# A hybrid mLSTM and sparse-attention block: the first stage's work in another order

## The chip, the core and the metric

The kernel runs on one core of a Trainium2 chip. The core has a matrix engine (TensorE, PE in the profile, with its weight loads as PEld), three engines for elementwise work (VectorE or DVE, ScalarE or ACT, GpSimd or POOL) and a queue for transfers (SyncE, SP). Each engine works through its own queue of instructions in order and waits on semaphores for the others. The time is device time in microseconds from one execution; the metric is the median of several executions.

## The reference

One decoder block of width 1024 on 512 tokens. It normalises the input, projects it with one wide matrix, and feeds the columns of that projection to two branches:

```
hN = rmsnorm(x, norm_g)
p  = split(hN @ w_in)          # m_q m_k m_v m_o m_z m_i m_f | n_q n_kc n_vc n_ks n_vs n_kw n_vw n_g n_z | g_a g_b
mLSTM branch:  conv + silu of q, k; chunkwise matrix memory with input gate m_i and forget gate m_f; layer norm
NSA branch:    compressed, selected and window attention over n_kc/n_vc, n_ks/n_vs, n_kw/n_vw, gated by n_g
merged = sigmoid(g_a) * (ya @ w_branch_a) + sigmoid(g_b) * (yb @ w_branch_b)
out    = rmsnorm(x + merged @ w_out, final_norm_g)
```

All tensors are float32. What matters here is the beginning: the norm of x, its transpose, and the projection onto a few narrow columns (n_vs, n_vw, n_g, m_i, m_f: 288 columns together).

## The kernel before

A float32 product is made of three products in a faster number format: each operand is split into a high part, which is the value rounded by a copy, and a low part, which is the value less its high part. `split` (line 129) does this with a copy on ACT and a subtraction on DVE. `mm3` (line 156) and `passes` (line 199) then issue high by high, high by low and low by high for every 128-row slice k of the contraction (eight slices, ND).

The first stage (lines 249 to 368) handles the 512 tokens in four blocks `tb` of 128. For each block:

- `stats(tb)`: ACT squares x and sums the squares (`ssq`), takes a logarithm (`ln`) and an exponential (`r`); one Newton step of four or five small instructions refines the inverse root, on DVE for block 0 and on POOL (lines 301 to 307) for the others.
- `transposed(tb)`: in two halves of 512 columns, DVE scales x in place by r and the norm's weight `gB` (tile `xt`), and TensorE transposes four slices into a bank of PSUM (tile `pt`, two banks).
- in the loop, `split` makes `hTh` (ACT) and `hTl` (DVE) from each half; `mm3` projects the block with 24 products of 288 columns (tile `pp`).
- `evacuate(tb, ps)` brings a finished projection out of PSUM: two pairs of an ACT copy and a DVE subtraction (tile `vsw`), then two DVE additions (tile `gp`) of biases.

The 288 columns of the weights arrive in tile `sraw` and are split two slices at a time by `small_split(k)` into `shi` and `slo`: for k = 0 and 4 POOL makes the high part and DVE the low part, for k = 2 and 6 ACT makes the high part and POOL the low part.

What sets the order: while the set `ordered` holds "act" and "dve", everything issued to those two engines keeps its order in the program; TensorE's, POOL's and SP's instructions are placed by a planner, which interleaves the transposes of the next block with the projection of the current one. The projection of block `tb` is issued after the next block's `transposed`, so on DVE the scaling of block tb + 1 stands ahead of `evacuate(tb - 1)`. After the stage `ordered.clear()` (line 368) hands ACT and DVE to the planner as well.

The loads of the first weights of the wide columns follow on SP's queue (line 143, tiles `wr`, `wh`, `wl`), each a job of the `Stream`: first two jobs for the compressed keys and values, then two for the selected and window keys. Behind them stand small transposes of parameters (L385, L386, L389), the angles of the rotary embedding (sine) and the forget gate's logarithm (tiles `fa`, `fe`, `fz`, `lf`). Tiles of the next stage reuse the memory of the first: the load of `w1t` (line 509), which the compression's first product (L537) reads together with `X`, waits until the last user of that memory is done.

Of the kernel before, what the change touches and what calls it, by code (L numbers as in the profile page):

```python
# [15 lines left out]
OP = mybir.AluOpType  # L16
# [4 lines left out]
NT = T // 128  # L21
ND = D // 128
# [41 lines left out]
def build(  # L64
# [4 lines left out]
    nc = tc.nc  # L69
# [17 lines left out]
    pe, pool = nc.tensor, nc.gpsimd  # L87
    act, dve = Engine(nc.scalar, "act"), Engine(nc.vector, "dve")
# [25 lines left out]
    ident = cst[:, CI : CI + 128]  # L114
# [41 lines left out]
    def mm3(ps, lh, ll, rh, rl, ks, start=True, stop=True):  # L156
        n = len(ks)
        for i, k in enumerate(ks):
            a, b, c, d = lh(k), ll(k), rh(k), rl(k)
            pe.matmul(ps, a, c, start=start and i == 0, stop=False)  # L160
            pe.matmul(ps, a, d, start=False, stop=False)  # L161
            pe.matmul(ps, b, c, start=False, stop=stop and i == n - 1)  # L162
# [71 lines left out]
    hTh = pers.tile([128, ND, T], F32R, name="hTh")  # L234
    hTl = pers.tile([128, ND, T], F32R, name="hTl")
# [13 lines left out]
    with tc.tile_pool(name="ph0", bufs=2, side="right") as p0, tc.tile_pool(  # L249
        name="small", bufs=1, side="right"  # L250
    ) as sp:
        SW = 288
        xts = [p0.tile([128, D], F32, name="xt", tag="xt", bufs=4) for _ in range(NT)]
# [7 lines left out]
        for k in (0, 4):  # L261
            ks = slice(k, k + 4)
# [9 lines left out]
        gB = []  # L272
        for hf in range(2):
            ps = PS()
            pe.matmul(ps, one, grow[:, hf * 512 : hf * 512 + 512], start=True, stop=True)
            gB.append(ps)
        shi = sp.tile([128, ND, SW], F32R, name="shi")
        slo = sp.tile([128, ND, SW], F32R, name="slo")

        def small_split(k):  # L280
            ks = slice(k, k + 2)
            if k % 4:
                A(shi[:, ks], raw[:, ks], AF.Copy)
# [3 lines left out]
            eng.tensor_tensor(slo[:, ks], raw[:, ks], f(shi[:, ks]), OP.subtract)  # L287

        epst = p0.tile([128, 1], F32, name="epst", bufs=1)
# [1 line left out]
        ssq = p0.tile([128, NT], F32, name="ssq", bufs=1)  # L291
        rs = []

        def stats(tb):
            sq = p0.tile([128, D], F32, name="sq", tag="sq", bufs=1)
            A(sq, xts[tb], AF.Square, accum_out=ssq[:, tb : tb + 1])
            v = p0.tile([128, 1], F32, name="v", tag="v", bufs=4)
            ln = p0.tile([128, 1], F32, name="ln", tag="ln", bufs=4)
            A(ln, ssq[:, tb : tb + 1], AF.Ln, bias=epst[:, 0:1], scale=1.0 / D)
            e = pool if tb else dve  # L300
# [3 lines left out]
            e.tensor_tensor(v, r, v, OP.mult)  # L304
            e.tensor_tensor(v, r, v, OP.mult)
# [19 lines left out]
        stats(0)  # L325

        def transposed(tb):
            xt, pts = xts[tb], []
            for hf in range(2):
                hs = slice(hf * 512, hf * 512 + 512)  # L330
                dve.scalar_tensor_tensor(xt[:, hs], xt[:, hs], rs[tb][:, 0:1], gB[hf], OP.mult, OP.mult)
                ps = PT()
                for k in range(4):
                    kk = hf * 4 + k
                    pe.transpose(ps[:, k * 128 : (k + 1) * 128], xt[:, kk * 128 : (kk + 1) * 128], ident)
                pts.append(ps.rearrange("p (k t) -> p k t", k=4))
            return pts

        pts = transposed(0)
        small_split(0)  # L340
        small_split(2)
        stats(1)
        last = None
        for tb in range(NT):
            ts = slice(tb * 128, (tb + 1) * 128)
            for hf in range(2):
                ks = slice(hf * 4, hf * 4 + 4)
                split(pts[hf], hTh[:, ks, ts], hTl[:, ks, ts])
                if tb == 0:
                    small_split(4 + 2 * hf)  # L350
# [11 lines left out]
            if tb == 0:  # L362
                nc.sync.dma_start(bif[:, 0:4], b_igate[0].partition_broadcast(128))
                nc.sync.dma_start(bif[:, 4:8], b_fgate[0].partition_broadcast(128))
                nc.sync.dma_start(bng, b_nsa_gate[0].partition_broadcast(128))
        stream.fetch()
        evacuate(NT - 1, last)
        ordered.clear()
# [14 lines left out]
        ps = PT()  # L383
# [13 lines left out]
        kk = sp.tile([128, 2, NT, 8], F32, name="kk")  # L397
# [277 lines left out]
    for src, dst in ((cpad, Ct), (spad, St)):  # L675
        ps = PT()
# [265 lines left out]
    for h in range(4):  # L942
# [54 lines left out]
        r = rsqrt(mp, va, NT, "rl")  # L997
# [26 lines left out]
    with tc.tile_pool(name="fin", bufs=1) as fp:  # L1024
# [106 lines left out]
```

## Time and profile before

| what | value |
|---|---|
| median of 3 runs | 645.48 us (644.75 to 646.33) |
| profiled execution | 644.24 us, its span 642.4 us |
| TensorE busy | 626.9 us, 98% of the span |
| VectorE, ScalarE, GpSimd busy | 411.5, 302.4, 54.0 us |
| granted TensorE clock, mean | 0.998 of full speed |
| bytes read from and written to memory | 55.01 MB, 2.10 MB |

The span runs from the first to the last instruction on the core; all times below that are not durations are counted from its start. In a row of the timeline stand the start, the duration, the engine, the line, the operation and the tiles written and read, with "xN" where N instructions are merged, and in brackets the idle time before them with what ended it. The chain of waits follows the work that ended last back from the end; its rows hold a start and the time that the step adds. L80 is the line of the helper through which all of ACT's and DVE's work passes, so their instructions are told apart by their tiles.

### The profile page before, as it was taken

How to read it: one execution, taken by the hardware profiler on the slowest of the kernel's cores; microseconds unless marked ns; L12 is line 12 of the kernel's file. 1: busy time of each engine (PE TensorE's matmuls, PEld its weight loads, DVE VectorE, ACT ScalarE, POOL GpSimd, SP SyncE). 2: the span in 40 equal slices, each digit the busy share in tenths (PEclk: the TensorE clock that was granted, in tenths of full speed). 3: DMA queues.
4: the chain of work that ended last, by engine and by line, in shares of the span. 5: the costliest groups of instructions: out<-in, count | busy, mean ns of one | idle time of the engine just before them, and what ended most of it. 6: DMA issues, size and time to landing. Idle time of an engine off the chain costs nothing.

```text
span 642.4 us, 9274 instructions
## 1 busy us (share of the span) xinstructions
PE 626.9 (98%) x3470; PEld 538.8 (84%) x3470; DVE 411.5 (64%) x878; ACT 302.4 (47%) x604; POOL 54.0 (8%) x114
## 2 busy tenths in 40 slices
PE   6999999999999999999999999999999999999995
PEld 4988788888878788888989889889888888888995
DVE  5796768767866865557669788696554233334455
ACT  5653554655655655435545546545322222223234
POOL 5000021121121231100000000000000000000000
PEclk9999999999999999999999999999999999999999
DMA  8476421122122212223313222232274242423203
GB/s 248 136 193 154 120 66 45 55 67 67 36 64 66 65 49 83 66 70 96 99 37 96 80 73 78 67 78 87 66 232 128 66 131 67 128 70 108 90 1 131
DMA packets 90124, 58.74 MB, mean 91 GB/s; under 512 B 4016, under 2 KB 86100, under 8 KB 90080
## 3 DMA queue, kind: packets, MB, share of 16 engines
q1 hardware_dynamic: 90080, 58.16, 31.8%
q8 instruction: 27, 0.44, 0.3%
q14 instruction: 17, 0.14, 0.1%
HBM read 55.01 MB, written 2.10 MB: 89 GB/s over the span
## 4 chain that ended last, share of the span: by engine, by line
PE 88%; DVE 7%; ACT 2%; DMA 1%; issue 1%; SPq 0%; POOL 0%; DVEq 0%; POOLq 0%
PE pp L204 21%; PE pp L202 21%; PE pp L206 21%; PE pp L162 3%; PE pp L160 3%; PE pp L161 3%; PE pt L784 2%; DVE wl L80 2%; PE po L797 1%; PE ps L769 1%; PE po L796 1%; PE ps L537 1%; ACT wh L80 1%; PE ps L770 1%; PE ps L162 1%
## 5 line engine op out<-in xcount | busy, mean ns | idle before, releaser
L202 PE MATMUL pp<-hTh,wh 128*128 128x512 f32 (+1 forms) x488 | 192.2, 394 | 0.0
L204 PE MATMUL pp<-hTl,wh 128*128 128x512 f32 (+1 forms) x488 | 191.3, 392 | 0.0
L206 PE MATMUL pp<-hTh,wl 128*128 128x512 f32 (+1 forms) x488 | 191.1, 392 | 0.0
L80 DVE TENSOR_TENSOR wl<-wr,wh 128x1024 fp32r<-128x1024 f32 x88 | 109.0, 1240 | 74.3 <-ACT wh L80 73.9
L80 ACT ACTIVATE wh<-wr 128x1024 fp32r<-128x1024 f32 x88 | 92.9, 1057 | 114.3 <-PE pp L204 82.8
L206 PEld LDWEIGHTS pp<-hTh,wl 128*128 128x128 f32 x488 | 91.8, 188 | 16.2
L202 PEld LDWEIGHTS pp<-hTh,wh 128*128 128x128 f32 x488 | 92.0, 188 | 15.3
L204 PEld LDWEIGHTS pp<-hTl,wh 128*128 128x128 f32 x488 | 92.0, 189 | 15.1
L778 POOL TENSOR_SCALAR P<-P,st 128x128 f32<-128x128 f32 (+1 forms) x64 | 38.5, 620 | 182.2 <-DVE st L80 134.1
L80 ACT ACTIVATE P<-P,st 128x128 f32<-128x128 f32 (+3 forms) x64 | 35.7, 558 | 36.6 <-DVE st L80 36.4
L80 DVE CUSTOM_DVE_ANT_0 P<-ps,cst 128x128 f32<-128x128 f32 (+3 forms) x64 | 30.4, 486 | 22.0 <-PE ps L770 21.6
L80 ACT ACTIVATE pth<-pt 128x512 fp32r<-128x512 f32 (+1 forms) x64 | 27.2, 434 | 29.8 <-PE pt L784 18.6
L80 DVE TENSOR_TENSOR ptl<-pt,pth 128x512 fp32r<-128x512 f32 (+1 forms) x64 | 30.4, 484 | 16.4 <-ACT pth L80 15.7
L204 PE MATMUL pp<-wl,hTh 128*128 128x256 f32 x128 | 36.2, 283 | 0.0
L206 PE MATMUL pp<-wh,hTl 128*128 128x256 f32 x128 | 36.2, 283 | 0.0
L202 PE MATMUL pp<-wh,hTh 128*128 128x256 f32 x128 | 36.2, 283 | 0.0
L161 PE MATMUL pp<-wl,meh 128*128 128x256 f32 x128 | 36.2, 283 | 0.0
L160 PE MATMUL pp<-wh,meh 128*128 128x256 f32 x128 | 36.2, 283 | 0.0
L162 PE MATMUL pp<-wh,mel 128*128 128x256 f32 x128 | 36.2, 284 | 0.0
L80 DVE SCALAR_TENSOR_TENSOR u<-pp,prm,u 128x511 f32<-128x511 f32 (+2 forms) x48 | 35.6, 742 | 0.4
L80 DVE SCALAR_TENSOR_TENSOR s<-s,pp 128x512 f32<-128x512 f32 x16 | 11.0, 687 | 29.5 <-PE pp L206 29.5
L784 PE MATMUL pt<-cst,P 128*128 128x128 f32 x160 | 28.6, 274 | 0.3 <-DVE ptl L80 0.3
(272 smaller groups left out, 1112.0 us busy)
## 6 DMA issues: line engine op xcount, KB each, us to landing
wr<-w_in SPq DMA_DIRECT2D x68, 512.0 KB, 3.9
wr<-w_branch_a SPq DMA_DIRECT2D x8, 512.0 KB, 3.8
wr<-w_out SPq DMA_DIRECT2D x8, 512.0 KB, 3.5
wr<-w_branch_b SPq DMA_DIRECT2D x4, 512.0 KB, 3.6
xo<-x SPq DMA_DIRECT2D x1, 2048.0 KB
out<-xo SPq DMA_DIRECT2D x8, 256.0 KB, 2.2
xt<-x SPq DMA_DIRECT2D x3, 512.0 KB, 5.8
k<-k SPq DMA_DIRECT2D x8, 128.0 KB, 2.3
```

The lines of the kernel that those rows point to most:

```text
L80: ins = fn(*args, **kw)
L160: pe.matmul(ps, a, c, start=start and i == 0, stop=False)
L161: pe.matmul(ps, a, d, start=False, stop=False)
L162: pe.matmul(ps, b, c, start=False, stop=stop and i == n - 1)
L202: pe.matmul(ps, a, c, start=k == 0, stop=False)
L204: pe.matmul(ps, a, d, start=False, stop=False)
L206: pe.matmul(ps, b, c, start=False, stop=k == nk - 1)
L537: pe.matmul(ph[:, :64], W1[i][:, j, :], Xs[i][:, j].rearrange("p g n -> p (g n)"), start=j == 0, stop=j == 15,)
L769: pe.matmul(pss[:, :n], tq, kh[:, b, :n], start=True, stop=False)
L770: pe.matmul(pss[:, :n], tq, kl[:, b, :n], start=False, stop=True)
L778: pool.tensor_scalar(pj, pj, st[:, 2, j : j + 1], 1.0, OP.mult, OP.mult)
L784: pe.transpose(pt[:, (qb - kb) * 128 : (qb - kb) * 128 + 128], P[:, POFF[qb] + kb * 128 : POFF[qb] + kb * 128 + 128], ident,)
```

## The change

Only the first stage is edited; loads, sizes and arithmetic stay.

- `small_split` becomes `small_hi` and `small_lo`, which are placed one by one. POOL makes the high part of k = 0 only; ACT makes those of k = 2, 4, 6. DVE makes the low parts of k = 0, 2, 4; POOL that of k = 6.
- `stats` becomes `square` and `inverse`. The second block's squares and inverse follow the first block's `hTh` on ACT; its inverse's small steps go to DVE instead of POOL.
- `project` issues the projection by ranges of k, and in each range all high-by-high products first, then high by low, then low by high. It and the transposes keep their order on TensorE.
- For block 0, four more transposes into an unused bank (`cold`) stand between the first half of the projection and the transposes of block 1.
- In the loop, TensorE gets the projection over k 0 to 3, the two transposes of the next block, then the projection over k 4 to 7. On ACT the next block's squares stand between the two halves of `hTh`. `evacuate(tb - 1)` stands ahead of the next block's scaling.

```diff
-        def small_split(k):
+        def small_hi(k, eng):
             ks = slice(k, k + 2)
-            if k % 4:
+            if eng == "a":
                 A(shi[:, ks], raw[:, ks], AF.Copy)
             else:
                 pool.tensor_scalar(shi[:, ks], raw[:, ks], 1.0, 1.0, OP.mult, OP.mult)
-            eng = pool if k % 4 else dve
+
+        def small_lo(k, eng):
+            ks = slice(k, k + 2)
             eng.tensor_tensor(slo[:, ks], raw[:, ks], f(shi[:, ks]), OP.subtract)
...
+        def project(ps, tb, ks):
+            ts = slice(tb * 128, (tb + 1) * 128)
+            for part in range(3):
+                for k in ks:
+                    l = (hTl if part == 2 else hTh)[:, k, ts]
+                    r = (slo if part == 1 else shi)[:, k, :]
+                    tc.keep_in_program_order(
+                        pe.matmul(
+                            ps[:, :SW], l, r, start=part == 0 and k == 0, stop=part == 2 and k == 7
+                        )
+                    )
+
+        square(0)
+        inverse(0, dve)
+        cold = PO()
+        pts = []
+        for hf in range(2):
+            scaled(0, hf)
+            pts.append(turned(0, hf))
+        small_hi(0, "p")
+        small_hi(2, "a")
+        small_lo(0, dve)
+        half(0, 0, pts[0])
+        small_lo(2, dve)
+        half(0, 1, pts[1])
+        square(1)
+        inverse(1, dve)
+        last = PP()
+        project(last, 0, range(4))
+        for k in range(4):
+            tc.keep_in_program_order(
+                pe.transpose(cold[:, k * 128 : (k + 1) * 128], xts[0][:, k * 128 : (k + 1) * 128], ident)
+            )
+        small_hi(4, "a")
+        small_hi(6, "a")
+        scaled(1, 0)
+        small_lo(4, dve)
+        scaled(1, 1)
+        small_lo(6, pool)
+        pts = [turned(1, 0)]
+        project(last, 0, (4, 5))
+        pts.append(turned(1, 1))
+        project(last, 0, (6, 7))
...
+        for tb in range(1, NT):
+            half(tb, 0, pts[0])
             if tb + 1 < NT:
-                pts = transposed(tb + 1)
-            if tb + 2 < NT:
-                stats(tb + 2)
-            if last is not None:
-                evacuate(tb - 1, last)
+                square(tb + 1)
+            half(tb, 1, pts[1])
+            if tb + 1 < NT:
+                inverse(tb + 1, pool)
+            evacuate(tb - 1, last)
             last = PP()
-            mm3(
-                last[:, :SW], lambda k: hTh[:, k, ts], lambda k: hTl[:, k, ts],
-                lambda k: shi[:, k, :], lambda k: slo[:, k, :], range(ND),
-            )
...
+            project(last, tb, range(4))
+            pts = []
+            if tb + 1 < NT:
+                for hf in range(2):
+                    scaled(tb + 1, hf)
+                    pts.append(turned(tb + 1, hf))
+            project(last, tb, range(4, 8))
         stream.fetch()
         evacuate(NT - 1, last)
         ordered.clear()
```

`scaled`, `turned` and `half` are the scaling, the four transposes and the split of one half of a block, taken out of `transposed` and the loop.

More of the change, by code (lines that the diff above doesn't have):

```diff
@@ L323, in evacuate @@
             dve.tensor_tensor(gp[:, tb, 24:32], ps[:, 280:288], bif, OP.add)
[L325 to L344, printed above, removed]
-            ts = slice(tb * 128, (tb + 1) * 128)
[L346 to L350, printed above, removed]
-            if tb + 1 < NT:
-                pts = transposed(tb + 1)
-            if tb + 2 < NT:
-                stats(tb + 2)
-            if last is not None:
-                evacuate(tb - 1, last)
-            last = PP()
-            mm3(
-                last[:, :SW], lambda k: hTh[:, k, ts], lambda k: hTl[:, k, ts],
-                lambda k: shi[:, k, :], lambda k: slo[:, k, :], range(ND),
-            )
[L362 to L365, printed above, removed]
+        def scaled(tb, hf):
+            xt, hs = xts[tb], slice(hf * 512, hf * 512 + 512)
+            dve.scalar_tensor_tensor(xt[:, hs], xt[:, hs], rs[tb][:, 0:1], gB[hf], OP.mult, OP.mult)
@@ new lines, in turned, with half @@
+        def turned(tb, hf):
+            ps = PT()
+            for k in range(4):
+                kk = hf * 4 + k
+                tc.keep_in_program_order(
+                    pe.transpose(
+                        ps[:, k * 128 : (k + 1) * 128], xts[tb][:, kk * 128 : (kk + 1) * 128], ident
+                    )
+                )
+            return ps.rearrange("p (k t) -> p k t", k=4)
+        def half(tb, hf, ps):
+            ts = slice(tb * 128, (tb + 1) * 128)
+            ks = slice(hf * 4, hf * 4 + 4)
+            split(ps, hTh[:, ks, ts], hTl[:, ks, ts])
@@ new lines, in build @@
+        square(0)
[15 more added lines that the diff above has]
+        project(last, 0, range(4))
+        for k in range(4):
+            tc.keep_in_program_order(
+                pe.transpose(cold[:, k * 128 : (k + 1) * 128], xts[0][:, k * 128 : (k + 1) * 128], ident)
+            )
@@ new lines, in build @@
+        small_hi(4, "a")
[8 more added lines that the diff above has]
+        project(last, 0, (6, 7))
+        nc.sync.dma_start(bif[:, 0:4], b_igate[0].partition_broadcast(128))
+        nc.sync.dma_start(bif[:, 4:8], b_fgate[0].partition_broadcast(128))
+        nc.sync.dma_start(bng, b_nsa_gate[0].partition_broadcast(128))
```

5 lines of the change are left out of this document (3 added, 2 removed).

## The prediction

> **What bounds the kernel now.** I read the page's chain first, then the busy time by stretches of the first 60 us, then the chain of waits and the timeline there, because the diff ends where the first stage ends.
>
> ```profile
> PE 88%; DVE 7%; ACT 2%; DMA 1%; issue 1%; SPq 0%; POOL 0%; DVEq 0%; POOLq 0%
> ```
> ```profile
> 8.40:11.80 3.40, 2.34 (x11) 1.79 (x10) 2.48 (x3) 3.10 (x7) 2.60 (x7) 1.00 1.11 377
> 11.80:15.20 3.40, 3.40 (x14) 3.12 (x14) 3.03 (x3) 1.72 (x5) 2.98 (x7) 1.00 0.53 155
> ...
> 18.60:28.70 10.10, 10.10 (x82) 10.10 (x81) 8.18 (x22) 6.10 (x15) 1.25 (x6) 1.00 0.29 88
> ...
> 35.50:47.40 11.90, 11.90 (x58) 9.68 (x56) 11.15 (x35) 6.26 (x11) 0.22 (x2) 1.00 0.74 198
> 47.40:60.00 12.60, 12.09 (x82) 10.97 (x81) 7.21 (x14) 4.86 (x7) 0.00 (x0) 1.00 0.64 160
> ```
> TensorE bounds the program. In the second fence (stretch, its length, then busy time of PE, PEld, DVE, ACT, POOL, the granted clock, DMA) PE is short of work from 8.4 to 11.8 (2.34 of 3.40 us) and has none to spare from 11.8 on: 10.10 of 10.10 us while blocks 1 to 3 are projected. So only two things can move the time: when TensorE's projections begin and run at full rate, and whether it stays fed.
>
> ```profile
> 8.63 1.16 ACT sq L80 x2
> 9.82 0.30 ACT ln L80
> 10.14 0.21 ACT r L80
> 10.49 0.20 POOL v L304
> 10.76 0.20 POOL v L305
> ...
> 12.21 0.24 PE pp L160
> ...
> 14.62 0.24 PE pp L161
> ...
> 15.57 0.13 PE pp L161
> ...
> 19.40 0.44 PE pt L335 x4
> ...
> 28.57 0.13 PE pp L160
> ```
> ```profile
> 7.96 1.97 PE L335 MATMUL pt<-cst,xt 128*128 128x128 f32 x8
> 10.98 0.58 PE L160 MATMUL pp<-shi,hTh 128*128 128x288 f32 x1 [1.06 <-POOL v L305]
> ...
> 17.23 0.29 PE L162 MATMUL pp<-shi,hTl 128*128 128x288 f32 x1
> ...
> 28.80 0.28 PE L202 MATMUL pp<-hTh,wh 128*128 128x256 f32 x1
> ```
> The chain of waits (start, duration) shows what holds the start: ACT runs the second block's squares (8.63), logarithm and exponential to 10.35 before hTh of block 0, though the eight transposes of block 0 are issued from 7.96 and over at 9.93. The first projection starts at 10.98. A 288-wide matmul is paced at 0.24 us there (12.21, still at 14.62) and at 0.13 from 15.57 to the end (28.57); the step lies near 15.2 us. Four transposes cost 0.44 us at the high rate. TensorE issues the 24th projection, all 16 transposes of blocks 0 and 1 being done, at 17.23, and the stage's successor (L202) at 28.80.
>
> **The change part by part.**
>
> *hTh of block 0 ahead of the squares.* The transposes leave the array's input free at about 9.7 and hTh is ready by then, so the first projection starts 1.3 us earlier, at 9.7. That is the whole gain on offer at this place. It does not last, by the rest of block 0:
>
> ```profile
> L80 DVE SCALAR_TENSOR_TENSOR xt<-xt,r,ps 128x512 f32<-128x512 f32 x8 | 5.7, 740 | 0.0
> L80 DVE TENSOR_TENSOR hTl<-pt,hTh 128x512 fp32r<-128x512 f32 x8 | 5.4, 688 | 1.6 <-ACT hTh L80 1.6
> L80 ACT ACTIVATE hTh<-pt 128x512 fp32r<-128x512 f32 x8 | 4.6, 593 | 2.9 <-PE pt L335 2.7
> ...
> L80 DVE TENSOR_TENSOR wl<-wr,wh 128x1024 fp32r<-128x1024 f32 x2 | 2.4, 1222 | 0.5 <-ACT wh L80 0.5
> ...
> L80 ACT ACTIVATE wh<-wr 128x1024 fp32r<-128x1024 f32 x2 | 2.0, 1052 | 0.0
> L80 ACT ACTIVATE shi<-sraw 128x576 fp32r<-128x576 f32 x2 | 1.4, 684 | 1.2 <-DMA sraw<-w_in 1.2
> ```
> ```profile
> 40.49 0.18 DVE L80 TENSOR_TENSOR fz<-fa,fz 128x16 f32<-128x16 f32 x1
> 40.70 0.17 DVE L80 SCALAR_TENSOR_TENSOR lf<-gp,fz 128x16 f32<-128x16 f32 x1
> ```
> The squares of block 1 now follow both hTh (from 9.0, 0.59 each with a little overlap): 10.4, plus 1.16, 0.30, 0.21 and hand-overs gives r at 12.1. The inverse is moved to DVE: four dependent steps at 0.21 (40.49 to 40.70) end at 12.9, the first half of xt (0.74) at 13.7. TensorE meanwhile has 12 projections at 0.24 and the four added transposes (0.21 each there, as 1.97/8 less the wait): 9.7 + 2.9 + 0.85 = 13.4. These four fill time it would wait in anyway; without that wait they cost 0.44 to 0.85. So the transposes of block 1 start at 13.7.
>
> *Low parts shared out anew.* slo of k = 2 goes to DVE (0.72, scaled from wl: 1222 x 576/1024), between the two hTl; DVE is otherwise waiting there, so nothing. Of the second half of the weights, ACT makes both high parts (12.0 to 13.3), DVE the low part of k = 4 (from 13.6), POOL that of k = 6 (from 13.3). These two collide:
>
> ```profile
> 8.17 1.41 POOL L287 TENSOR_TENSOR slo<-sraw,shi 128x576 fp32r<-128x576 f32 x1
> ...
> 8.55 1.65 DVE L80 TENSOR_TENSOR slo<-sraw,shi 128x576 fp32r<-128x576 f32 x1
> ```
> Beside POOL's 1.41 us subtraction, DVE's own took 1.65 us and ended 0.62 after POOL's end: it did next to nothing while POOL ran. I take this: slo of k = 4 ends at 15.3 (alone it would be 14.3), the second half of xt at 16.0, its transposes start there, and after six projections block 0 is finished at 17.3. [...] Against 17.23 plus 0.13 of before, the early start is used up: gain about 0.1 us.
>
> *The loop's new order.* TensorE's queue now holds, per block: the projection over k 0 to 3, both transposes of the next block, the projection over k 4 to 7. On DVE the evacuation of the block before (vsw twice, gp twice) stands ahead of the next block's xt; before, it stood behind.
>
> ```profile
> 25.83 0.28 ACT L80 ACTIVATE vsw<-pp 128x128 fp32r<-128x128 f32 x1 [0.86 <-PE pp L162]
> ...
> 27.07 0.15 DVE L80 TENSOR_TENSOR gp<-pp,bif 128x8 f32<-128x8 f32 x1
> ```
> An evacuation takes 1.39 us from ACT's start to the last gp (25.83 to 27.22). Block 0 ends at 17.4 on TensorE; ACT, still busy with r of block 2, begins at 17.6; gp ends at 19.0, xt at 19.6, transposes can start at 19.7. TensorE has 12 projections of 0.132 for that time and is through at 18.85: it waits 0.8, and 0.2 more for the second half of xt. (POOL's inverse, five steps of 0.27 by 10.49 and 10.76, ends at 18.6: next in line, not last.) Block 1 ends at 22.4; there ACT has block 3's squares between the two hTh, so its evacuation begins at 22.8; xt ends at 24.8, TensorE is free at 23.9: 0.9 and 0.2. Block 2 has nothing to transpose for. Sum: 17.3, plus three blocks of 24 x 0.132 = 9.5, plus 16 transposes at 0.11 = 1.8, plus 1.0 and 1.1 of waiting: 30.7. Before issues the same point at 28.80. The stage costs 1.9 us more, where 18.60:28.70 showed no wait at all.
>
> *What stands behind the stage.* No line there is edited, but the planner orders it anew.
>
> ```profile
> 31.95 0.66 PE L385 MATMUL pt<-cst,rows 11*128 11x11 f32 x8
> ...
> 32.67 0.39 PE L204 MATMUL pp<-hTl,wh 128*128 128x256 f32 x1
> ...
> 47.10 0.39 PE L206 MATMUL pp<-hTh,wl 128*128 128x512 f32 x1
> 48.00 3.76 PE L537 MATMUL ps<-X,w1t 128*128 128x64 f32 x32 [0.51 <-DVE Z L80]
> ```
> ```profile
> 30.61 1.28 ACT L80 ACT_TABLE_LOAD   x1
> ...
> 32.32 0.22 ACT L80 ACTIVATE fe<-fa 128x16 f32<-128x16 f32 x1
> ```
> ```profile
> 41.15 0.88 SPq L509 DMA_DIRECT2D w1t<-cmp_w_k  x1
> ```
> ```profile
> SPq L509 <- DVE lf L80: 2.6, 1, 2.6
> ```
> The small transposes (0.72 us, 31.95 to 32.67) move from inside the first column job to ahead of it: no change in sum. They also cover wl of that job, which is late with the stage (wh behind block 2's evacuation, 28.6 to 29.6, wl to 30.9); without that cover it would cost 0.2. The loads keep their order on SP's queue, past which nothing is moved; the first two weight loads wait for no engine. TensorE then reaches L537, ready before at 47.3 (47.10 plus 0.23), at 49.1. Before, it waited there until 48.00. The load of w1t, for which SP's queue waited 2.6 us on lf, is issued 0.28 us after it (40.87 to 41.15), and L537 follows that issue by 6.85 us. The page names Z on DVE as the releaser, 47.87; both are possible. In the new order lf comes later than the stage alone explains: the sine with its table load goes ahead of the forget gates' exponential, which gets a load of its own. Gates wait for the last gp (34.6), then load 1.28, sine, load 1.28: fe ends at 38.1, where before it ended at 32.54. From there DVE has five small steps, the wl of the fourth weights (1.22) and 16 more steps at 0.21: lf ends at 43.8. If L537 waits for the load, it starts at 43.8 + 0.28 + 6.85 = 50.9, 2.9 later than before; if it waits for Z and X on DVE, whose chain I put at 49.1, it starts at 49.2, 1.2 later. I take 2.8, because SP's issue follows lf so closely and the load has by far the longer way. From there to the end the queues hold the same work in the same order but for a few small steps, and TensorE 88% of the chain, so the delay is carried to the end.
>
> Sum: +2.8 us (1.9 from the stage, 0.9 from the load). The profiled execution took 644.24 us, its span 642.4; it lies 1.24 under the median of the runs, 645.48. So 647.0 for a like execution, 648.3 as the median. Ends: the unknown prices run from +0.5 (Z decides L537, DVE wins the port, which gives back up to 0.7) to +2.9, and the clock can add 1.4.
>
> **The rivals.**
>
> *The projections stay fed (faster).* If the evacuation ended within 0.84 us of a block's end (12 projections, 1.58, less xt, 0.74), the transposes would never wait. [...] For it: the second fence shows the gap in 8.40:11.80. Against it: 1.39 us for an evacuation is measured, and in-order DVE must do it first. [...]
>
> [...]
>
> [...]
>
> **How the numbers follow.** 0.3% is 1.9 us, about what a measurement of this kernel can tell from no change. The forecast has 0.64 (its own range +2.0 to +3.6: 647.5 to 649.1), fed projections 0.12, the late clock 0.08, the smaller sum 0.16. Slower by over 0.3%: 0.64 and 0.08, 0.72. Within: 0.16. Faster: 0.12. The range leaves out the faster case and a little above the late clock: 645.8 to 650.4.
>
> **What would show it.** Right: the first projection at 9.7; transposes of xt that wait for DVE xt at some 13.7, 16.0, 19.7, 24.8, about 1 us each in blocks 1 and 2; the first L202 job at 31.4 after the small transposes; w1t issued near 44.1. Wrong: PE fully busy from 13 to 28, or the evacuation's vsw done before TensorE has finished the half projection; L537 starting within 0.2 us of the job before it, which would leave 1.2.

## The result and the profile after

| what | before | changed |
|---|---|---|
| median of 13 executions each | 645.53 us (644.51 to 646.33) | 647.71 us (647.04 to 651.13) |
| profiled execution, its span | 644.24 us, 642.4 | 647.15 us, 645.3 |
| ratio of the times | | 1.0052, 95% interval 1.0040 to 1.0063 |

The changed kernel is slower by 0.5%, a difference that is small but clear of the interval. Its 13 executions fall into two groups: eight of 647.04 to 647.81 us at a mean granted clock of 0.997 or 0.998, and five of 650.29 to 651.13 us at 0.993 or 0.994. The profile is one of the first group; the experiments show where the second comes from.

Busy time by stretches of the changed kernel (stretch, its length, then busy time of PE, PEld, DVE, ACT, POOL, the granted clock, DMA share and GB/s):

```profile
8.40:11.80 3.40, 3.40 (x16) 3.08 (x15) 2.72 (x6) 2.61 (x6) 0.00 (x0) 1.00 1.11 378
11.80:15.20 3.40, 2.68 (x15) 2.16 (x13) 3.10 (x7) 2.23 (x5) 1.41 (x1) 1.00 0.49 139
...
18.60:28.70 10.10, 8.47 (x63) 7.64 (x63) 6.82 (x17) 4.56 (x12) 1.45 (x7) 1.00 0.26 74
...
47.40:60.00 12.60, 11.33 (x67) 9.68 (x66) 7.47 (x15) 2.06 (x5) 0.00 (x0) 1.00 0.88 224
```

The gap that stood in 8.40:11.80 is closed, and two others have opened: TensorE is busy for 8.47 of 10.10 us where it had no wait at all, and for 11.33 of 12.60 around the product with w1t. The timeline of TensorE names them (start, duration, instruction, in brackets the wait and what ended it):

```profile
9.62 1.30 PE L355 MATMUL pp<-shi,hTh 128*128 128x288 f32 x4
...
11.67 1.16 PE L355 MATMUL pp<-shi,hTl 128*128 128x288 f32 x4
12.63 1.00 PE L379 MATMUL po<-cst,xt 128*128 128x128 f32 x4
13.58 0.63 PE L337 MATMUL pt<-cst,xt 128*128 128x128 f32 x4
...
15.23 0.53 PE L355 MATMUL pp<-slo,hTh 128*128 128x288 f32 x2 [0.75 <-DVE slo L80]
...
15.98 0.63 PE L337 MATMUL pt<-cst,xt 128*128 128x128 f32 x4
...
17.24 0.69 PE L355 MATMUL pp<-shi,hTh 128*128 128x288 f32 x4
...
19.72 1.33 PE L337 MATMUL pt<-cst,xt 128*128 128x128 f32 x8 [0.73 <-issue]
...
24.98 1.33 PE L337 MATMUL pt<-cst,xt 128*128 128x128 f32 x8 [0.75 <-issue]
...
31.71 0.39 PE L202 MATMUL pp<-hTh,wh 128*128 128x256 f32 x1
...
49.15 0.39 PE L206 MATMUL pp<-hTh,wl 128*128 128x512 f32 x1
50.80 3.76 PE L581 MATMUL ps<-X,w1t 128*128 128x64 f32 x32 [1.27 <-DMA w1t<-cmp_w_k]
```

The first projection comes 1.36 us earlier than before, yet block 1's starts at 17.24, where before the last one of block 0 was issued at 17.23. Four transposes take 1.00 us at 12.63 and 0.63 at 13.58: the pace rises in between. That this is a step of the clock is my estimate from the durations alone, since the granted-clock column is 1.00 in all these stretches; the profile without the four transposes has the same low pace, 0.24 us a product (two from 17.40 to 17.88, here four from 11.67 to 12.63), in a stretch with a granted clock of 0.60. Block 1's second four come at 15.98, behind the wait of 0.75 for slo, which is the missing part of 11.80:15.20 (2.68 of 3.40). In the two rows of eight transposes, 0.28 us more of waiting stands inside, ahead of the second four (1.33 for eight that take 1.04 where nothing is late). L581 is what L537 was before; it starts 2.80 us later, and the spans differ by 2.9.

What the waits are for, in the timeline of POOL and DVE:

```profile
13.15 1.41 POOL L289 TENSOR_TENSOR slo<-sraw,shi 128x576 fp32r<-128x576 f32 x1 [5.19 <-ACT shi L80]
...
18.63 0.19 POOL L310 TENSOR_TENSOR r<-r,v 128x1 f32<-128x1 f32 x1
```
```profile
13.39 1.78 DVE L80 TENSOR_TENSOR slo<-sraw,shi 128x576 fp32r<-128x576 f32 x1
15.10 0.73 DVE L80 SCALAR_TENSOR_TENSOR xt<-xt,r,ps 128x512 f32<-128x512 f32 x1
...
18.81 0.16 DVE L80 TENSOR_TENSOR gp<-pp,bif 128x8 f32<-128x8 f32 x1
18.88 1.40 DVE L80 SCALAR_TENSOR_TENSOR xt<-xt,r,ps 128x512 f32<-128x512 f32 x2
```

And in the chain of waits, the load behind lf, 6.62 us from issue to landing:

```profile
43.56 0.19 DVE lf L80
...
43.94 6.62 DMA w1t<-cmp_w_k
...
50.80 3.76 PE ps L581 x32
```

### The profile page after: what moved, and what is told of

Same layout as the page of the kernel before. It is cut to its first block, busy times and chain, and to the rows that moved or that the text cites. A ratio compares the mean times of both kernels' runs of the same rounds, so it can differ in the third digit from the quotient of the medians.

```text
span 645.3 us, 9280 instructions
## 1 busy us (share of the span) xinstructions
PE 627.9 (97%) x3474; PEld 539.1 (84%) x3474; DVE 412.9 (64%) x884; ACT 302.4 (47%) x605; POOL 50.6 (8%) x107
## 4 chain that ended last, share of the span: by engine, by line
PE 86%; DVE 8%; ACT 3%; issue 2%; DMA 1%; SPq 0%; DVEq 0%; ACTq 0%
PE pp L202 21%; PE pp L204 21%; PE pp L206 20%; PE pp L162 2%; PE pp L161 2%; PE pp L160 2%; PE pt L828 2%; DVE wl L80 2%; PE po L841 1%; PE ps L813 1%; ACT wh L80 1%; PE pp L355 1%; PE po L840 1%; PE ps L581 1%; PE ps L814 1%
## 5 line engine op out<-in xcount | busy, mean ns | idle before, releaser
L202 PE MATMUL pp<-hTh,wh 128*128 128x512 f32 (+1 forms) x488 | 192.4, 394 | 0.0
L202 PEld LDWEIGHTS pp<-hTh,wh 128*128 128x128 f32 x488 | 92.0, 188 | 15.3
L202 PE MATMUL pp<-wh,hTh 128*128 128x256 f32 x128 | 36.2, 283 | 0.0
```

The lines of the kernel that those rows point to most:

```text
L202: pe.matmul(ps, a, c, start=k == 0, stop=False)
```

## The experiments

The theory at the start (A): TensorE waits for xt behind the evacuation in blocks 1 and 2, and w1t's load waits for the late lf; the early start is lost in block 0 to the two subtractions that collide. Its rival: the clock alone. Every run was measured beside the kernel before, in five sessions, in which that kernel's median lay between 645.07 and 645.53 us. So times of runs from different sessions can differ by some 0.5 us for no reason of the kernel; where it matters I also give the distance to the kernel before of the same session, in which the short executions of the changed kernel stand at +1.8 us.

**xt ahead of the evacuation.** One part of the loop's order undone in the changed kernel.

```diff
+            if tb + 1 < NT:
+                for hf in range(2):
+                    scaled(tb + 1, hf)
             evacuate(tb - 1, last)
...
                 for hf in range(2):
-                    scaled(tb + 1, hf)
                     pts.append(turned(tb + 1, hf))
```

> The changed kernel, with one part undone: inside the loop both halves of the next block's xt stand ahead of the evacuation on DVE again, as before the change. Theory A (mine: in blocks 1 and 2 TensorE waits some 1 us each for xt behind the evacuation, and the load of w1t behind lf adds the rest): the transposes in those blocks wait for nothing, the first stage ends some 2 us sooner, first L202 job at about 29.7 instead of 31.7; lf keeps its own extra table load, so the load of w1t gains at most the 2 us of the stage; time 1.5 to 2.2 us below the changed kernel, 645.5 to 646.2, level with before. Theory B (the added time is the clock's step alone, which comes late in part of the executions): the profiled time does not move by more than 0.3 us, only the share of long executions does. Theory C (only the load of w1t counts, stage hidden): the stage ends sooner but L581's column product starts where it did, within 0.3 us, and the time is that of the changed kernel.

Measured: 652.02 us (647.85 to 653.54), ratio to before 1.0093 (1.0066 to 1.0119). Nothing was gained: the two short executions, 647.85 and 648.00, lie above those of the changed kernel. Timeline of this kernel:

```profile
17.69 0.69 PE L355 MATMUL pp<-shi,hTh 128*128 128x288 f32 x4
...
20.14 1.33 PE L337 MATMUL pt<-cst,xt 128*128 128x128 f32 x8 [0.71 <-issue]
```
```profile
19.30 1.41 DVE L80 SCALAR_TENSOR_TENSOR xt<-xt,r,ps 128x512 f32<-128x512 f32 x2 [0.89 <-POOL r L310]
```

The transposes follow the start of block 1's projection by 2.45 us, as in the changed kernel (17.24 to 19.72, 2.48). DVE now waits for r: the next block's logarithm and exponential stand behind the second hTh on ACT, and POOL's steps behind them end when the evacuation would have ended. So the theory had half of the cause. (Block 0 was 0.45 us late in this execution, as ACT waited until 9.10 for the load of the small weights; the wait for w1t grew to 1.51 us, and four of the six executions were of the long kind.)

**The forget gate ahead of the sine.** ACT makes gates, fa and fe first, so fe needs no table load behind the sine (1.28 us at 36.72 in the changed kernel).

```diff
-        A(sc, ang, AF.Sin)
+        tc.keep_in_program_order(A(gates, gp[:, :, 0:24], AF.Tanh, scale=0.5))
+        tc.keep_in_program_order(A(fa, gp[:, :, 28:32], AF.Abs))
+        tc.keep_in_program_order(A(fe, fa, AF.Exp, scale=-1.0))
+        tc.keep_in_program_order(A(sc, ang, AF.Sin))
```

> The changed kernel, with the gates' Tanh, the Abs and the Exp of the forget gate ahead of the sine on ACT, so that fe needs no table load behind the sine. Theory A (lf releases the load of w1t, and that load the column product L581): fe ends some 2.5 us sooner (from 38.2 to about 35.7), lf at about 41 to 42, the load of w1t is issued right behind it, and L581 starts up to 1.27 us sooner, as the product has waited 1.27 for the load: time 0.9 to 1.3 us below the changed kernel, 646.4 to 646.8. The sine comes later, and if its tables (cpad, spad) are wanted soon, part of this is given back. Rival (Z and X on DVE, not the load, release L581): the load is issued sooner, the product starts where it did, time unchanged within 0.2.

Measured: 645.83 us (645.72 to 646.74), ratio to before 1.0014 (1.0005 to 1.0023): 1.5 below the short executions of the changed kernel (their median is 647.31), or 1.1 by the distances to the kernel before (+0.7 here, +1.8 there), which is what was expected. None of the 11 is long. ACT's and SP's timelines:

```profile
35.22 0.22 ACT L80 ACTIVATE fe<-fa 128x16 f32<-128x16 f32 x1
```
```profile
42.63 0.88 SPq L553 DMA_DIRECT2D w1t<-cmp_w_k  x1
```

The load is issued 1.31 us earlier, and L581 starts at 49.46, with no wait that the chain or the waits name. It follows the issue of the load by 6.83 us, as L581 of the changed kernel did (43.94 to 50.80, 6.86): the load moved and the product moved with it, so in the changed kernel the product waited for the load and not for Z and X.

**Without the four added transposes.** Their result is read by nobody.

```diff
-        for k in range(4):
-            tc.keep_in_program_order(
-                pe.transpose(cold[:, k * 128 : (k + 1) * 128], xts[0][:, k * 128 : (k + 1) * 128], ident)
-            )
```

> The changed kernel without the four added transposes of block 0 whose result nobody reads (they cost 0.85 us of TensorE between the first 12 projections and block 1's transposes). Theory A: they fill time in which TensorE waits for xt anyway, so the time in block 0 is unchanged within 0.2 us, and the clock steps up where it did (about 13.3); time within 0.5 us of the changed kernel. [...] Rival port: without them the second set of projections gets nothing sooner; a gain of over 0.3 us would say that they delay block 1's transposes.

Measured: 648.19 us (647.17 to 653.33), ratio 1.0065 (1.0039 to 1.0091). The profiled execution, 651.38 us, was a long one, and its stretches show the granted clock (third figure from the right) drop twice:

```profile
15.20:18.60 3.40, 3.31 (x15) 3.16 (x16) 1.98 (x4) 1.72 (x5) 0.39 (x3) 0.60 1.05 304
...
47.40:60.00 12.60, 11.28 (x52) 9.86 (x52) 8.48 (x16) 3.03 (x7) 0.00 (x0) 0.74 0.96 250
```

The second drop stands behind the wait for w1t (1.32 us here). That gave a new theory: the long executions come from that wait, and the first stage can have a drop of its own.

**POOL's subtraction moved to DVE.**

```diff
-        small_lo(6, pool)
+        small_lo(6, dve)
```

> The changed kernel with the low part of the small weights' rows k = 6, 7 on DVE behind that of k = 4, 5, and POOL left out of it. Theory A (the two subtractions exclude each other: DVE's took 1.78 us beside POOL's 1.41): DVE's first takes about 0.75, the second half of xt ends at about 14.1 instead of 15.1 if the subtraction of k = 6 stands behind it, TensorE's wait of 0.75 us at 15.2 goes, and block 0 ends 0.5 to 0.9 us sooner; the evacuation of block 0 follows it, so the time falls by 0.4 to 0.8 us, to 646.9 to 647.3 for the short executions. Rival (a sum on one engine: DVE now has 1.5 us of its own in place of 1.78): the last low part on DVE ends about where it did, and the time is unchanged within 0.3 us.

Measured: 649.46 us (646.22 to 649.97), ratio 1.0053 (1.0035 to 1.0071); the two short executions, 646.22 and 646.53, lie 0.9 below those of the changed kernel, or 0.5 by the distances to the kernel before. Two executions are too few to size a gain of this kind. The timeline of TensorE and the stretches:

```profile
11.72 0.69 PE L355 MATMUL pp<-shi,hTl 128*128 128x288 f32 x4
...
15.07 0.63 PE L337 MATMUL pt<-cst,xt 128*128 128x128 f32 x4
...
16.34 0.69 PE L355 MATMUL pp<-shi,hTh 128*128 128x288 f32 x4
...
50.13 4.84 PE L581 MATMUL ps<-X,w1t 128*128 128x64 f32 x32 [1.35 <-DMA w1t<-cmp_w_k]
```
```profile
50.00:53.40 3.40, 3.27 (x26) 3.30 (x27) 3.08 (x6) 0.13 (x1) 0.00 (x0) 0.88 1.09 279
53.40:56.80 3.40, 3.40 (x13) 3.01 (x13) 1.07 (x5) 0.48 (x2) 0.00 (x0) 0.50 1.12 265
56.80:60.20 3.40, 3.40 (x11) 2.65 (x11) 0.00 (x0) 0.00 (x0) 0.00 (x0) 0.62 0.00 1
```

The wait for slo is gone (DVE's two subtractions take 0.75 us each, at 13.52 and 14.84), the second four transposes come at 15.07 instead of 15.98, and block 1 starts 0.9 us sooner (16.34): that is what the collision cost in block 0. The pace of TensorE rose earlier in this execution (0.69 us for four products at 11.72), but that did not bring block 1 forward, since its first transposes wait for xt and come at 13.70, as late as in the changed kernel (13.58). This profile is of a long execution: behind the wait of 1.35 us the granted clock is at half rate (0.50 in 53.40:56.80) from about 52.6, for 3.40 x (0.12 + 0.50 + 0.38) x 2 = 6.8 us, which would cost half of that, 3.4. In the profile of the short kind, the changed kernel's, the wait is there too (1.27) and the clock stays at 1.00.

**Both parts of the loop undone,** on the kernel with the forget gate first: xt ahead of the evacuation as above, and the statistics a block earlier.

```diff
         small_hi(6, "a")
+        square(2)
+        inverse(2, pool)
...
-            if tb + 1 < NT:
-                square(tb + 1)
+            if tb + 2 < NT:
+                square(tb + 2)
...
-            if tb + 1 < NT:
-                inverse(tb + 1, pool)
+            if tb + 2 < NT:
+                inverse(tb + 2, pool)
```

> The kernel with the forget gate ahead of the sine (645.8, first L202 job at 31.80), and in the loop two parts undone together: the statistics of the next block (squares, logarithm, exponential, POOL's steps) come one block earlier, as before the change, and both halves of xt stand ahead of the evacuation on DVE. Theory A2 (formed after the run with xt first alone, where xt waited 0.89 twice for POOL's r instead of the evacuation): two chains end within 0.3 us of each other, so both have to go; now xt of the next block starts right behind hTl, the transposes wait for nothing, the first L202 job comes at 29.8 to 30.0, and the time is 643.7 to 644.2. It is less where the load of w1t is last again, because the planner puts a wh ahead of fe here: then L581 waits up to 1 us, the time is 644.4 to 645 and part of the executions is some 3 us longer. Rival (the order on TensorE itself, transposes between two half projections, is what costs): waits of 0.5 us and more stay ahead of the transposes of blocks 2 and 3, the stage gains under 0.5 us, time 645.3 to 645.8.

Measured: 644.66 us (644.43 to 647.79), ratio to before 0.9998 (0.9988 to 1.0007). Timeline of TensorE:

```profile
18.80 1.23 PE L337 MATMUL pt<-cst,xt 128*128 128x128 f32 x8
...
23.05 1.04 PE L337 MATMUL pt<-cst,xt 128*128 128x128 f32 x8
...
28.69 0.28 PE L202 MATMUL pp<-hTh,wh 128*128 128x256 f32 x1
...
48.15 3.76 PE L585 MATMUL ps<-X,w1t 128*128 128x64 f32 x32 [0.79 <-DVE X L80]
```
```profile
41.23 0.88 SPq L557 DMA_DIRECT2D w1t<-cmp_w_k  x1
```

Both waits are gone. The first L202 comes at 28.69 (the small transposes stand behind it here); in the kernel with the forget gate first, on which this one is built, the instruction behind the projections started at 31.09: 2.4 us. Of that 0.8 is lost again to a wait ahead of the product, and the time fell by 1.2, to the less good of the two outcomes that the expectation named. The profile names X for that wait, but the product follows the issue of the load by 6.92 us (41.23 to 48.15), as in every kernel here whose product has a wait (6.80 to 6.96 in eight of them, the kernel before among them), so it is the load again. One of 11 executions is long.

**The statistics alone** a block earlier, the evacuation still ahead of xt (the edit shown above, without that of xt, also on the kernel with the forget gate first).

> The kernel with the forget gate ahead of the sine (645.8), and of the loop's two parts only the statistics come one block earlier; the evacuation stays ahead of xt on DVE. Theory A2 (two chains of nearly equal length, both needed): xt of block 2 still starts behind gp at about 18.9, the first wait stays at about 0.7 plus 0.3, the second falls by at most 0.4, since logarithm and exponential of the next block no longer stand ahead of that evacuation on ACT; time 645.4 to 645.9. Rival (the statistics alone set the waits, the evacuation never counted): as with both undone, 644.4 to 644.9.

Measured: 645.73 us (645.58 to 646.57), ratio 1.0011 (1.0002 to 1.0020): no gain either, as in the run with xt alone. DVE goes from the last gp straight to xt:

```profile
19.34 0.16 DVE L80 TENSOR_TENSOR gp<-pp,bif 128x8 f32<-128x8 f32 x1
19.42 1.40 DVE L80 SCALAR_TENSOR_TENSOR xt<-xt,r,ps 128x512 f32<-128x512 f32 x2
```

Two chains of nearly equal length led to xt, and only undoing both frees it.

**lf later, in the kernel before.** The first stage is untouched; five idle steps delay lf.

```diff
         dve.tensor_tensor(fz, fa, fz, OP.mult)
+        for n in range(5):
+            dve.tensor_scalar(fz, fz, 1.0, None, OP.mult)
```

> The kernel before, with five more dependent steps (a multiplication by 1.0 on 128x16, 0.21 us each) in the chain of the forget gate ahead of lf, so that the load of w1t is issued some 1.05 us later; the first stage is untouched. Theory clock (a wait of over some 1.2 us in front of the product with w1t makes the granted clock fall to half for some 6.6 us in part of the executions): the product waits about 1.5 us, short executions take 646.0 to 646.3 and a part, from a fifth to two thirds, takes some 3.3 us more, at a mean clock of about 0.993. Rival (the long executions belong to the changed first stage and its clock): all executions lie at 646.0 to 646.4, none is longer. Second rival (the load is not what the product waits for in the kernel before): time unchanged at 645.1.

Measured: 649.87 us (645.87 to 651.89), ratio 1.0063 (1.0039 to 1.0086). Two executions are short (645.87, 646.62), five long (649.63 to 651.89, clock 0.991 to 0.993).

```profile
12.37 0.58 PE L160 MATMUL pp<-shi,hTh 128*128 128x288 f32 x1 [2.61 <-POOL v L305]
...
50.27 3.76 PE L539 MATMUL ps<-X,w1t 128*128 128x64 f32 x32 [1.51 <-DMA w1t<-cmp_w_k]
```

With a wait of 1.51 us at this place in the profile, five executions of seven are long without any of the change in the first stage. The rival that ties them to the changed first stage falls. (The late first projection of this profile is taken up in the run after next.)

**w1t freed from lf, in the changed kernel.** gp and the gate's four small tiles lie in memory that the load does not reuse.

```diff
-        gp = sp.tile([128, NT, 32], F32, name="gp")
+        gp = np_.tile([128, NT, 32], F32, name="gp")
...
-        fa = sp.tile([128, NT, 4], F32, name="fa")
+        fa = np_.tile([128, NT, 4], F32, name="fa")
```
(and the same for fe, fz, fq)

> The changed kernel, with gp and the four small tiles of the forget gate (fa, fe, fz, fq) in the pool that lives on through the branch, so that neither the load of w1t nor Z waits until lf has read them; same instructions. Theory A (late lf costs through the space of w1t alone): the load is issued at about 41 instead of 43.9, L581 starts when TensorE gets there (49.2) instead of 50.8, the wait of 1.27 goes, time 1.2 to 1.5 us below the short executions of the changed kernel, 645.8 to 646.1, and no execution is 3 us longer. Rival (the long executions come from the clock's first step in the first stage): the short ones gain, but about 4 in 10 are still some 3 us longer. Rival (lf's own users come next): the wait moves to another place behind L581 and the time gains under 0.5 us.

Measured: 645.65 us (645.46 to 646.38), ratio 1.0010 (1.0002 to 1.0019). None of 11 is long, and the time is 1.7 below the short executions of the changed kernel, or 1.2 by the distances to the kernel before. SP issues the load 6.2 us earlier, well before the 41 expected, and TensorE finds it there:

```profile
37.76 0.88 SPq L553 DMA_DIRECT2D w1t<-cmp_w_k  x1
```
```profile
49.46 3.68 PE L581 MATMUL ps<-X,w1t 128*128 128x64 f32 x32
```

**The same in the kernel before.**

```diff
-        gp = sp.tile([128, NT, 32], F32, name="gp")
+        gp = np_.tile([128, NT, 32], F32, name="gp")
...
```

> The kernel before, with gp and the four tiles of the forget gate in the pool that lives on, nothing else. Theory A: the wait of 0.51 ahead of the product with w1t (48.00) goes, as the load and Z no longer wait for lf: time 0.4 to 0.6 us below before, 644.5 to 644.7. Rival (the product waits for Z and X, which DVE makes no sooner as it is busy with wl and the gate's small steps): unchanged, 644.9 to 645.2.

Measured: 644.63 us (643.62 to 645.36), ratio 0.9993 (0.9984 to 1.0002). The wait of 0.51 us is gone from the profile; the gain has the size expected, but its interval touches none. Its first stage is that of the kernel before, and so is that of the run with lf later, yet the first projection starts at 11.50 and 12.37 in their profiles, where the profile of the kernel before has 10.98:

```profile
11.50 0.58 PE L160 MATMUL pp<-shi,hTh 128*128 128x288 f32 x1 [1.68 <-POOL v L305]
```

ACT starts on the small weights, for whose load it waits, at 7.89 and 8.67 instead of 7.40, and the first L202 comes at 29.64 and 30.09 instead of 28.80. So the profile of the kernel before shows an early execution.

**hTh of block 0 ahead of the squares, alone,** in the kernel before.

```diff
-        stats(1)
...
                 split(pts[hf], hTh[:, ks, ts], hTl[:, ks, ts])
+                if tb == 0 and hf == 1:
+                    stats(1)
```

> The kernel before, with the one step that the change is named after: the second block's squares and inverse are issued behind both hTh of block 0; all else, the loop's order too, stays. Theory A: the first projection starts at 9.7 instead of 10.98, and after 18 projections at the low rate (4.3 us) TensorE stands at about 14.0 in front of the transposes of block 1, whose xt is not earlier than before, since r of block 1 comes 1 us later; the gain is eaten up there but for what an earlier step of the clock gives, and the time is 0 to 0.6 us below before, 644.5 to 645.1. Rival (the projections stay fed): the whole 1.3 us arrives, 643.8. Rival (r is later than its cover): xt of block 1 comes a microsecond later than in the kernel before, and the time is 0.5 to 1 us above it.

Measured: 644.71 us (644.34 to 645.33), ratio 0.9994 (0.9985 to 1.0003): no difference that can be told.

```profile
9.64 0.58 PE L160 MATMUL pp<-shi,hTh 128*128 128x288 f32 x1
...
15.54 1.06 PE L335 MATMUL pt<-cst,xt 128*128 128x128 f32 x4
...
29.16 0.28 PE L202 MATMUL pp<-hTh,wh 128*128 128x256 f32 x1
```

The projection starts at 9.64, and the stage ends at 29.16, not before the 28.80 of the kernel before, which is an early execution. Here TensorE has work from 11 on without a wait and does it at the low rate, 0.24 us a product, until about 16. How much of the late end is this rate and how much xt was not taken apart.

**w1t freed, without the four transposes,** in the changed kernel.

```diff
-        for k in range(4):
-            tc.keep_in_program_order(
...
-        gp = sp.tile([128, NT, 32], F32, name="gp")
+        gp = np_.tile([128, NT, 32], F32, name="gp")
...
```

> The kernel with gp and the gate's tiles out of the way of w1t (645.65, no long executions), without the four added transposes. It takes the wait for w1t out of the run without them, in which two clock effects stood together. Theory clock in block 0: in part of the executions the granted clock, just risen at about 13.3, falls back in front of block 1's second transposes, as in the profile without the four (half rate from 15.7 to 19.0), and those take some 1.0 us more: executions at 645.6 and at 646.6 or above. Theory A (the transposes only fill time): all executions within 645.4 to 646.4, as with them. Rival (they cost time): all below 645.3.

Measured: 645.74 us (644.83 to 646.97), ratio 1.0008 (0.9993 to 1.0022). Five executions lie at 646.63 to 646.97, five at 645.56 to 645.74, one at 644.83; with the four transposes nine of 11 lay below 645.9 and two at 646.3 to 646.4. So without them about half of the executions take 1.0 us more. The four cost nothing that the traces show: block 1's first transposes start at 13.67 without them and at 13.70 with them, because xt comes no sooner. That they hold the clock up in block 0 is inferred, not shown. It rests on the size: the drop at 15.20:18.60 (granted clock 0.60) in the run without them moved the transposes of block 2 from 19.72 to 20.76. This kernel's own profile is of a short execution, in which the granted clock stays at 1.00 through a wait of 1.59 us:

```profile
13.67 0.63 PE L337 MATMUL pt<-cst,xt 128*128 128x128 f32 x4 [1.59 <-issue]
```
```profile
11.80:15.20 3.40, 1.18 (x9) 0.73 (x7) 3.00 (x7) 2.21 (x5) 1.41 (x1) 1.00 0.47 147
```

**All that helped, together:** both parts of the loop undone, the forget gate first, w1t freed, POOL left out.

```diff
-        small_lo(6, pool)
+        small_lo(6, dve)
...
+            if tb + 1 < NT:
+                for hf in range(2):
+                    scaled(tb + 1, hf)
             evacuate(tb - 1, last)
...
-        A(sc, ang, AF.Sin)
+        tc.keep_in_program_order(A(gates, gp[:, :, 0:24], AF.Tanh, scale=0.5))
...
```

> All that helped together: both parts of the loop undone, the forget gate ahead of the sine, gp and its four tiles in the pool that lives on, and the low part of k = 6, 7 on DVE. Theory A2: against the kernel with both parts undone (644.5 to 644.7) block 0 ends 0.9 sooner, as it did when POOL was left out (16.34 instead of 17.24), and L585's wait of 0.79 for X goes; the sum is 1.7, of which the wait goes in full only where X comes sooner too: 642.8 to 643.5, all executions within 1 us, faster than before by 0.2 to 0.35 in a hundred. Rival (the early start cannot be kept, whatever is freed, because the loads or ACT are next): 644.3 to 645, no different from before.

Measured: 643.62 us (643.03 to 643.89), ratio to before 0.9972 (0.9963 to 0.9981). That is just above the range expected (642.8 to 643.5). No execution is long; it beats both kernels, by 1.5 us the one before and by 4.1 us the changed one, whose median its long executions raise. The first L202 comes at 28.79 although the load of the small weights let the first projection start only at 10.21 in this execution, and the product with w1t needs no wait:

```profile
47.30 3.68 PE L585 MATMUL ps<-X,w1t 128*128 128x64 f32 x32
```

## Why the prediction was right, point by point

- *The start.* Forecast 9.7, measured 9.62; the rest of block 0 used it up as said: xt of block 1 at 12.73 + 0.75, slo on DVE 1.78 long beside POOL's 1.41, block 1's projection at 17.24 (forecast 17.3). POOL did get ahead, by 0.24 us. The range has 0.7 us for DVE ahead of POOL; no run shows this term. What they show is DVE's subtraction at 1.78 us beside POOL's and 0.75 without it, and 0.9 us given back in block 0 when POOL was left out.
- *The loop.* Forecast waits of 0.8 and 0.2, then 0.9 and 0.2; measured 0.73 and 0.28, 0.75 and 0.28. The first L202 job came at 31.71 (31.4). The cause was told half: the evacuation does end last (gp 18.97, xt 18.88 to 20.28), but POOL's inverse, put down as "next in line, not last", ends 0.15 us before it, and moving either alone gains nothing.
- *Behind the stage.* fe ends at 38.23 (forecast 38.1), lf at 43.74 (43.8), the load at 43.94 (44.1), L581 at 50.80 (50.9). The 2.80 us split into 2.05 for the stage (the last product ahead of it starts at 49.15, before at 47.10) and 0.75 for the load; I had 1.9 and 0.9. The load, not Z, releases the product, in the kernel before too, where the page of the profile names Z: from issue to product it took 6.85 us there and 6.86 here. The smaller sum, 1.2 with Z as the releaser, falls with it.
- *The sum.* 2.8 forecast, 2.9 between the profiled executions. The step to the median was mis-sized: I added the 1.24 us by which the profiled execution lay below its median. The executions of the kernel before spread over 2 us (644.2 to 646.5 in nearly all of 101) and its profile is from the bottom, with an early first projection, while the changed kernel's lies 0.16 below the median of its eight short executions. These are 1.8 above the median of before, not 2.8; the five long ones, 4.8. That the median of all, 647.71, lies in the forecast's own range of 647.5 to 649.1 is therefore in part luck: the short executions alone have 647.31, and the long ones, for which the sum had no term, lift it.
- *The late clock.* The range has 1.4 us, and the chances 0.08, for a clock that rises later because of the waits in block 0; no run shows this term. What the runs show is a drop of the clock at another place, behind the wait for w1t. It decided, as I infer, the time of five executions in 13, by 3.0 us (650.36 against 647.31, the groups' medians): their mean clock is 0.993 or 0.994, and the profiles of two other kernels have a granted clock of 0.50 there for about 6.8 us, but no profile of these five was kept. The step that failed is the price of that wait: I gave it 0.9 us and nothing for what goes with it in the clock. In block 0 a drop was seen too (granted clock 0.60 in 15.20:18.60), worth 1.0 us, but only in a kernel without the four added transposes.
- *Fed projections.* They need both undone parts of the loop; then the stage is 2.4 us shorter, and it ends no sooner than before (28.69 against 28.80 in an early execution of before), since the early start is lost in block 0 all the same.

## What to carry to other kernels

An early start is worth what the next late thing leaves of it: follow each moved step to the wait that ends last behind it, and look for a second chain that ends at the same time before undoing one. A load that waits for memory hangs on the last reader of anything in that memory, here a scalar chain that no line of the diff touches; moving 768 bytes per partition brought the load from 43.94 to 37.76 and took the wait of 1.27 us away. And a wait on TensorE can go with a price beyond its length: with that wait of 1.27 us in the profile, five executions of 13 took 3.0 us more, and without it none of 11. One profile shows neither that nor whether its execution was an early or a late one: read several executions and their clocks.

## What the runs showed of the hardware

The length of one wait on TensorE, ahead of the product with w1t, and the share of executions some 3 us or more longer than the shortest group, at a clock of 0.994 or less:

| wait in the profile, us | kernels | long executions |
|---|---|---|
| none named | forget gate first, statistics early, freed (four kernels) | 0 of 65 |
| 0.50 to 0.51 | before, and hT first | 1 of 101, 0 of 11 |
| 0.79 | both parts undone | 1 of 11 |
| 1.27 | changed | 5 of 13 |
| 1.32 | without the four transposes | 2 of 6 |
| 1.35 | POOL left out | 4 of 6 |
| 1.51 | xt first; lf later | 4 of 6; 5 of 7 |

All the waits in this table end with the landing of the same load, so only its lateness was varied. In the two profiles of long executions, without the four transposes and with POOL left out, the granted clock is at 0.50 for about 6.8 us, from some 1.5 and 2.5 us behind the end of the wait. Of the other long executions only the time and the mean clock are known: the profiled one of the kernel without POOL, with this drop alone, has a mean of 0.994 where short ones have 0.997, and most of the others show 0.993 or 0.994 too. The groups' medians lie 3.0 us apart in the changed kernel, 3.2 without POOL and 4.1 with lf later; 6.8 us at half rate would cost 3.4, by my estimate. With waits of 1.27 to 1.51 us in the profile, 20 executions of 38 were long. The length alone does not decide it: a gap of 1.59 us in block 0 passed at a clock of 1.00 in the kernel with w1t freed and without the four transposes, and so did gaps of 0.73 and 0.75 us in the changed kernel's loop. A safe length can't be read from these runs. The point in block 0 at which the pace of TensorE rises was not the same in two profiles: with the same work up to there, four products from 11.67 took 1.16 us in the changed kernel (where the pace rises near 13.3), and from 11.72 only 0.69 in the kernel without POOL.

What stays open: which feature of the wait or of the small products behind it (64 columns each) decides that the clock drops; why some long executions are 5 us longer rather than 3 (up to 653.54 in the kernel with xt first); and one long execution of the kernel before (649.28), whose wait is only 0.5 us.
